# Gates and merges with tokens on the partitions, values behind the transposes, and a first product block tile by tile

## The chip, the core and the metric

The kernel runs on one core of a Trainium2 chip. Its metric is the device time of one execution in microseconds (us); the runs shown give 966.24, 966.26 and 968.72 us, median 966.26. The engines are named as in the profile: PE (TensorE, matmul), PEld (its weight load), DVE (VectorE), ACT (ScalarE), POOL (GpSimd) and SP (SyncE, which issues most DMAs).

## The reference, cut to what matters

Two transformer blocks stand one behind the other, on 256 tokens of width 1024, in float32. What the change touches:

```python
# block 1
z = rms_norm(x, norm1_w) @ w_in
(q, k_c, v_c, k_s, v_s, k_w, v_w, g_nsa, xr, gr, g_a, g_b) = split(z)
attn = nsa_attention(...)          # 8 heads: compressed, selected and windowed keys, gated
rnn  = rg_lru_branch(xr, gr, ...)  # conv, gates, scan over time, times gelu(gr)
merged = sigmoid(g_a) * (attn @ w_up_attn) + sigmoid(g_b) * (rnn @ w_up_rnn)
x = x + merged @ w_out             # then a feed-forward: square(relu(h @ mlp_w1)) @ mlp_w2
# block 2
h = h + 0.5 * swiglu(...)
qa, ka, va, qb, kb, vb, ga, gb = split(rms_norm(h) @ w_in_2)
ya = neighbourhood_attention_2d(qa, ka, va, rpb);  yb = windowed_gqa_sink(rope(qb), rope(kb), vb)
merged = sigmoid(ga) * (ya @ w_branch_a) + sigmoid(gb) * (yb @ w_branch_b)
h = h + merged @ w_out_2           # then a second swiglu and the last norm
```

## The kernel before

**Number format.** Each float32 operand is split in two parts of the fast matmul type, high and low: a copy on ACT gives the high part, a subtraction on DVE the low one (`split2`, L325; for weights `split_to`, L248 and L249). A product is then three matmuls, high by high, high by low and low by high. Weights arrive in pieces of up to 1024 columns (`raw`), are split into `whi` and `wlo` (five buffers each), and a piece is split two pieces ahead of its use (`wt`, L253). A buffer comes free when the last matmul that reads it is done.

**Layout.** Activations lie feature-major: 128 features on the partitions, 256 tokens along the free axis. `mmx` (L296) holds a weight tile of 128x128 and streams 256 tokens, three times. `mm3` (L290) is the other way about: a tile of activations (128 features by 128 tokens) is held and up to 512 weight columns are streamed, so that tokens come out on the partitions; before, the last down projection `ld` (L1483), `va` and `vg` use it. `mm_wide` (L302) streams high and low tokens together (512 columns) and then 256 for the low weights; the big feed-forwards and `wo` use it.

**Order.** Steps are recorded in the order of two lists, `ORDER_1` and `ORDER_2`, and a scheduler then sets the final order on each engine, which is fixed from there on. An entry such as `ga0` is one pair of output tiles of the gate g_a; `kv0` and `q0` are the first products of block 1; `ma0`..`mb3` are the two up projections; `at1` takes one attention step from a queue (scores, or transposes with the values straight behind them). Gates are evacuated by DVE (L984, times the norm's reciprocal), then go through tanh on ACT (L985). The merge multiplies (L1044), adds (L1050) and splits (L1051) each pair of tiles. PSUM is divided into pools: `g` three banks, `s` two, `t` two, `o` one.

**Start.** `setup` (L428) issues the DMA of the norm weights `vec` on ACT's queue, x in three DMAs and the first weight chunks between them on SP, and runs three warm-up matmuls `hot`. SP reuses eight DMA semaphores in turn, so a ninth DMA goes out when the first has landed.

Of the kernel before, what the change touches and what calls it, by code (L numbers as in the profile page):

```python
# [23 lines left out]
EARLY = 6  # L24
# [4 lines left out]
class Plan:  # L29
# [159 lines left out]
class Prog:  # L189
# [15 lines left out]
    def prepare(self):  # L205
# [32 lines left out]
    def split_to(self, i):  # L238
        nc = self.nc
        while self.n_split <= min(i, len(self.plan.pieces) - 1):  # L240
# [8 lines left out]
            nc.vector.tensor_tensor(out=lo[:, :w], in0=src, in1=hi[:, :w].bitcast(F32), op=ALU.subtract)  # L249
# [86 lines left out]
    def fm(self, tag, name, nk, npair, x, evac, rows=None, cols=None, lead=2, hold=2, after=None):  # L336
# [38 lines left out]
def build(nc, tc, d, out, es, dbg=None):  # L375
# [52 lines left out]
    def setup():  # L428
# [4 lines left out]
        for _ in range(3):  # L433
            nc.tensor.matmul(hb, hot[:, :P], hot, start=True, stop=True)
# [25 lines left out]
        for k in range(8):  # L460
            G.split2(*S["u0"].tile(k), res[:, k, :], V["norm1"][:, k:k + 1])
# [80 lines left out]
    def norm0():  # L542
        G.split_to(5)
        G.load_to(4)
        G.behind(nc.sync.dma_start(out=keep("ident", (P, P)), in_=d["ident"]), G.raw_ins[4])
        for p in range(4):
# [4 lines left out]
            G.behind(ins, G.hi_ins[5])  # L551
# [55 lines left out]
    def set_consts():  # L607
        G.load_to(6)
        G.behind(nc.sync.dma_start(out=S["vec2"], in_=d["vec2"]), G.raw_ins[6])
        G.behind(constants("cst1", CONST_1), G.raw_ins[6])  # L610

    def vg():
# [6 lines left out]
        hc = G.small((P, 2), "halfcol")  # L619
        nc.vector.tensor_scalar(out=hc, in0=S["colA"], scalar1=0.5, scalar2=None, op0=ALU.mult)  # L620
# [260 lines left out]
    def rnn_prep():  # L881
# [4 lines left out]
        nc.vector.tensor_tensor(out=tb, in0=ta, in1=V["lam"], op=ALU.min)  # L886
# [92 lines left out]
    def ev_tanh(key):  # L979
        def ev(p, b):  # L980
            if p == 0:
                S[key] = G.big(key)
# [599 lines left out]
```

## Time and profile before

| what | value |
|---|---|
| median of three runs | 966.26 us |
| the profiled execution | 966.17 us |
| its span, first to last instruction | 964.4 us |
| PE busy | 948.3 us, 98% of the span |
| DVE busy | 728.4 us, 76% |
| ACT busy | 585.0 us, 61% |

The difference of 1.8 us between the profiled time and its span lies outside the instructions. Busy is not idle-free work: a matmul's record is longer than the distance to the next one, since they are pipelined, so the cost of a matmul is read from start to start.

### The profile page before, as it was taken

What the parts mean: (1) busy time and instruction counts of PE and PEld (TensorE: products, weight loads), DVE (VectorE), ACT (ScalarE), POOL (GpSimd) and SP (SyncE); (2) the same over time, 40 slices, a digit from 0 to 9 for tenths busy, and PEclk for the clock granted to TensorE, in tenths of its full rate; (3) what the DMA queues carried; (4) which work ended last, traced back from release to release, by engine and by line L of the source; (5) the groups of instructions that cost most, each with busy time, mean ns of one, the idle gap of its engine ahead of it and who ended that gap; (6) DMA issues with size and microseconds to landing.
All of it is one profiled execution on the core that took longest, in us unless ns stands there. A gap on an engine that the chain in (4) does not pass through costs nothing.

```text
span 964.4 us, 15990 instructions
## 1 busy us (share of the span) xinstructions
PE 948.3 (98%) x6310; PEld 870.1 (90%) x6310; DVE 728.4 (76%) x1219; ACT 585.0 (61%) x961; POOL 42.0 (4%) x71
## 2 busy tenths in 40 slices
PE   8999999999999999999999999899999999999997
PEld 7989999998888888888888889899999888888897
DVE  7898879879888655679888657779767878777553
ACT  6795898546767544566555445678764565555441
POOL 6100000000000000030000200000000000000000
PEclk9999999999999999999999999999999999999999
DMA  9575442634545555565555755353334565555541
GB/s 331 188 268 212 138 154 104 245 131 178 215 175 193 201 177 196 195 207 180 203 187 182 240 180 177 136 204 108 113 132 172 178 201 204 185 175 183 186 141 45
DMA packets 26556, 174.03 MB, mean 180 GB/s; under 512 B 3313, under 2 KB 3569, under 8 KB 7281
## 3 DMA queue, kind: packets, MB, share of 16 engines
q1 hardware_dynamic: 24912, 169.80, 49.8%
q0 software_dynamic: 1136, 2.63, 1.4%
q8 instruction: 49, 0.80, 0.3%
q10 hardware_dynamic: 432, 0.58, 0.2%
q14 instruction: 27, 0.21, 0.1%
HBM read 171.43 MB, written 1.05 MB: 179 GB/s over the span
## 4 chain that ended last, share of the span: by engine, by line
PE 93%; ACT 4%; DVE 1%; issue 1%; DMA 0%; POOL 0%; POOLq 0%; ACTq 0%
PE f L306 17%; PE w L306 12%; PE f L307 9%; PE w L307 6%; PE ld L294 6%; PE ga L300 5%; PE fd L306 4%; PE gb L300 4%; PE wo L306 3%; PE m1b L300 2%; PE fd L307 2%; PE xr L300 2%; PE gr L300 2%; PE wo L307 2%; PE va L294 1%; PE ka L300 1%
## 5 line engine op out<-in xcount | busy, mean ns | idle before, releaser
L249 DVE TENSOR_TENSOR wlo<-raw,whi 128x1024 fp32r<-128x1024 f32 (+3 forms) x322 | 389.1, 1210 | 168.0 <-ACT whi L248 150.3
L248 ACT ACTIVATE whi<-raw 128x1024 fp32r<-128x1024 f32 (+3 forms) x322 | 335.7, 1047 | 285.6 <-PE w L306 64.2
L306 PE MATMUL f<-u,whi 128*128 128x512 f32 x704 | 246.7, 396 | 0.0
L307 PE MATMUL f<-u,wlo 128*128 128x256 f32 x704 | 196.5, 279 | 0.0
L306 PEld LDWEIGHTS f<-u,whi 128*128 128x128 f32 x704 | 132.0, 188 | 31.3
L307 PEld LDWEIGHTS f<-u,wlo 128*128 128x128 f32 x704 | 132.7, 188 | 0.1
L306 PE MATMUL w<-u,whi 128*128 128x512 f32 x256 | 88.8, 392 | 0.0
L306 PE MATMUL w<-hid,whi 128*128 128x512 f32 x256 | 88.8, 391 | 0.0
L307 PE MATMUL w<-hid,wlo 128*128 128x256 f32 x256 | 71.7, 280 | 0.0
L307 PE MATMUL w<-u,wlo 128*128 128x256 f32 x256 | 71.3, 280 | 0.0
L306 PE MATMUL fd<-f1h,whi 128*128 128x512 f32 x176 | 61.1, 394 | 0.0
L294 PE MATMUL ld<-whi,f2h 128*128 128x256 f32 (+1 forms) x264 | 59.0, 319 | 0.0
L306 PEld LDWEIGHTS w<-hid,whi 128*128 128x128 f32 x256 | 47.9, 187 | 10.5
L306 PEld LDWEIGHTS w<-u,whi 128*128 128x128 f32 x256 | 47.7, 187 | 10.3
L300 PE MATMUL ga<-u,whi 128*128 128x256 f32 x256 | 48.2, 284 | 1.1 <-ACT whi L248 1.1
L307 PE MATMUL fd<-f1h,wlo 128*128 128x256 f32 x176 | 48.8, 277 | 0.0
L307 PEld LDWEIGHTS w<-u,wlo 128*128 128x128 f32 x256 | 48.3, 189 | 0.2
L307 PEld LDWEIGHTS w<-hid,wlo 128*128 128x128 f32 x256 | 48.4, 189 | 0.0
L300 PE MATMUL gb<-u,whi 128*128 128x256 f32 x256 | 48.2, 284 | 0.0
L294 PEld LDWEIGHTS ld<-whi,f2h 128*128 128x128 f32 x264 | 44.0, 191 | 3.4
L306 PE MATMUL wo<-m,whi 128*128 128x512 f32 x128 | 44.3, 393 | 0.0
L294 PE MATMUL ld<-wlo,f2h 128*128 128x256 f32 (+1 forms) x132 | 42.1, 319 | 0.0
(533 smaller groups left out, 1924.5 us busy)
## 6 DMA issues: line engine op xcount, KB each, us to landing
raw<-in_ws_dram SPq DMA_DIRECT2D x150, 1024.0 KB, 4.8
raw<-in_ws_dram SPq DMA_DIRECT2D x3, 960.0 KB, 4.8
raw<-in_ws_dram SPq DMA_DIRECT2D x2, 992.0 KB, 4.9
nar<-in_rpb_dram POOLq DMA_DIRECT2D x16, 96.0 KB, 6.0
raw<-in_ws_dram SPq DMA_DIRECT2D x4, 256.0 KB, 6.4
raw<-in_ws_dram SPq DMA_DIRECT2D x2, 512.0 KB, 7.0
raw<-in_ws_dram SPq DMA_DIRECT2D x1, 932.0 KB, 5.1
res<-in_x_dram SPq DMA_DIRECT2D x2, 384.0 KB, 6.2
```

Source lines behind the costliest of these rows:

```text
L248: self.hi_ins.append(nc.scalar.activation(out=hi[:, :w], in_=src, func=AF.Copy))
L249: nc.vector.tensor_tensor(out=lo[:, :w], in0=src, in1=hi[:, :w].bitcast(F32), op=ALU.subtract)
L294: mm(out, a, b, start=start and r == 0, stop=stop and r == 2, skip_group_check=True)
L300: mm(out, a, b, start=start and r == 0, stop=stop and r == 2, skip_group_check=True)
L306: mm(bank.rearrange("p (a t) -> p a t", a=2), wh, x, start=start, stop=False, skip_group_check=True)
L307: mm(bank[:, :T], wl, x[:, 0, :], start=False, stop=stop, skip_group_check=True)
```

## The change

**Token-major gates and merges.** `tok` replaces the feature-major products of all four gates and all four up projections: an activation tile is held and 512 weight columns are streamed, tokens come out on the partitions. `ev_gate` needs no multiplication by DVE: the norm's reciprocal is a column per token and goes into ACT's tanh as its scale, straight from PSUM. In a part that ends a sum, the four weight tiles are held for both token halves (first all k of tokens 0 to 127, then all k of 128 to 255). The merged result must be turned back to feature-major for `wo`: 32 transposes on PE in all (16 per block), in `turn`; the split reads the turned tiles from PSUM. Half of a turn stands before the first product of `wo`, the other half (`mid`) between its later products; `wo` starts three pairs of output tiles instead of two before it closes the first.

**First products.** `kv0` and `q0` become one step, `first`, that goes through the eight k tiles and takes all four weight tiles of each; x and the weights come in eight DMAs each, alternating; the first weight chunk is issued on ACT's queue, `vec` on SP; the warm-up is two matmuls of 512 and 384 columns instead of three of 512. Tile 0 of `u0` (x times the norm weight) is split by DVE alone.

**Values behind transposes.** The attention queues take transposes and values as steps of their own, the values one or more steps later (`pv` in block 1, `v` in block 2).

**Other parts.** `qa` takes its PSUM banks from pool `s` instead of `g`; the mask of the neighbourhood bias becomes a step of its own (`nb`); a few small copies before the reciprocal root are dropped.

```diff
-EARLY = 6
+EARLY = 8
...
-ORDER_1 = """kv0 norm q0 cst kv_fin xr0 k0 q1 xr1 cmp_x cw0 cw1 cw2 vg0 cw3 prep cw4 at1 cw5 ga0 cw6 cw7 xr2 cmp_hT cmp_fin cmp_w2
...
+ORDER_1 = """norm cst xr0 kv_fin q_fin k0 q1 xr1 cmp_x cw0 cw1 cw2 vg0 cw3 prep cw4 at1 cw5 ga0 cw6 ga1 cw7 xr2 cmp_hT cmp_fin cmp_w2
+xr3 at1 ga2 cmp_attn ga3 at3 gr0 lru0 lru1 lru2 lru3 at1 gr1 at1 gr2 pv0 at1 gr3 exp sqrt bt at1 gelu gb0 pv0 at1 scan0 at1
+gb1 scan1 gb2 scan2 at2 scan3 gb3 at1 mb0 at1 mb1 pv0 at1 mb2 pv0 mb3 ma0 ma1"""
+ORDER_2 = """qs0 qs1 qe0 qe1 nb ka0 ka1 at1 va qb0 at1 qb1 at2 kb at3 ga0 at3 ga1 at3 ga2 at3 ga3 at3 gb0 at2 gb1 at2 gb2 at1
+ma0 gb3 ma1 mb0 mb1"""
...
+            if ci >= EARLY or ci % 4 == 0:
+                pool = "big" if ci < EARLY else "raw"
+                t = self.pools[pool].tile([P, 2 * PIECE], F32, tag=pool, name=f"raw{ci}")
+            else:
+                t = self.raw[ci - 1][:, PIECE // 2:]
+            queue = self.nc.sync if ci else self.nc.scalar
+            self.raw_ins.append(queue.dma_start(out=t[:, :w], in_=self.d["ws"][o:o + P * w].rearrange("(p w) -> p w", p=P)))
+            if ci > 1:
...
         if lead > 1 and hold:
             for p in range(lead):
                 part(p, 0, nk - hold)
+                if mid and p == 1:
+                    self.step(mid)
             for p in range(lead):
                 part(p, nk - hold, nk)
...
-        for _ in range(3):
-            nc.tensor.matmul(hb, hot[:, :P], hot, start=True, stop=True)
+        for n in (512, 384):
+            nc.tensor.matmul(hb[:, :n], hot[:, :P], hot[:, :n], start=True, stop=True)
...
-        nc.scalar.dma_start(out=vec, in_=d["vec"])
-        nc.sync.dma_start(out=res[:, 0:2, :], in_=d["x"][:, 0:2, :])
-        G.load_to(0)
-        nc.sync.dma_start(out=res[:, 2:5, :], in_=d["x"][:, 2:5, :])
-        G.load_to(1)
-        nc.sync.dma_start(out=res[:, 5:8, :], in_=d["x"][:, 5:8, :])
-        G.load_to(2)
+        nc.sync.dma_start(out=vec, in_=d["vec"])
+        for k in range(8):
+            nc.sync.dma_start(out=res[:, k:k + 1, :], in_=d["x"][:, k:k + 1, :])
+            G.load_to(k)
...
+            h, l = S["u0"].tile(k)
+            w = V["norm1"][:, k:k + 1]
+            if k:
+                G.split2(h, l, res[:, k, :], w)
+                continue
+            nc.vector.tensor_scalar(out=h, in0=res[:, k, :], scalar1=w, scalar2=None, op0=ALU.mult)
+            nc.vector.scalar_tensor_tensor(out=l, in0=res[:, k, :], scalar=w, in1=h.bitcast(F32), op0=ALU.mult, op1=ALU.subtract)
...
+    def tok(tag, name, c0, nk, x, ev, rows=None):
+        rows = rows or (lambda k: [(k * P, P)])
+        st = {}
+        def part(n):
+            c, h = divmod(n, nk // 4)
+            ks = range(4 * h, 4 * h + 4)
+            end = ks[-1] == nk - 1
+            def fn():
+                if h == 0:
+                    st[c] = [G.ps("g", f"{tag}{c}{i}") for i in range(2)]
+                ws = {k: G.wt((tag, k, c)) for k in ks} if end else None
+                for k, i in ([(k, i) for i in range(2) for k in ks] if end else [(k, i) for k in ks for i in range(2)]):
+                    wh, wl = ws[k] if end else G.wt((tag, k, c))
+                    xh, xl = (a[:, i * P:(i + 1) * P] for a in x(k))
+                    G.mm3(st[c][i], wh, wl, xh, xl, k == 0, k == nk - 1)
+                    if k == nk - 1:
+                        ev(c, i, st[c][i])
+            G.step(fn, [((tag, k, c), name, rows(k), [(c0 + c * 512, 512)]) for k in ks])
+        return part
...
+    def ev_gate(key, hc):
+        def ev(c, i, b):
+            if key not in S or S[key, "of"] != hc:
+                S[key] = G.big(key, shape=(P, 2, D))
+                S[key, "of"] = hc
+            nc.scalar.activation(out=S[key][:, i, c * 512:(c + 1) * 512], in_=b, func=AF.Tanh, scale=S["half" + hc][:, i:i + 1])
...
+    def take_values():
+        br, j = values.pop(0)
+        if br:
+            G.step(lambda: [nsa_cmp_pv(e) for e in (j - 1, j)])
+        G.step(lambda: nsa_pv(br, j // 2))
+        if br:
+            G.step(lambda: nsa_out(j // 2))
...
+    def first():
...
+            S["kcvc"], S["q0"] = G.ps("g", "kcvc0"), G.ps("s", "q0")
+            for k in range(8):
+                ws = [(S[key][:, nn * T:(nn + 1) * T], *G.wt((tag, k, nn)), nn) for key, tag in (("kcvc", "kcvc"), ("q0", "q"))
+                      for nn in range(2)]
+                x = xu(k)
+                for o, wh, wl, nn in ws:
+                    for a in range(2):
+                        nc.tensor.matmul(o, wh, x[:, a, :], start=k + nn + a == 0, stop=False, skip_group_check=True)
+                for o, wh, wl, nn in ws:
+                    nc.tensor.matmul(o, wl, x[:, 0, :], start=False, stop=k == 7, skip_group_check=True)
...
+        def ev(key):
+            def fn(c, i, b):
+                t = S[key][:, i, c * 512:(c + 1) * 512]
+                nc.vector.scalar_tensor_tensor(out=t, in0=t, scalar=1.0, in1=b, op0=ALU.add, op1=ALU.mult)
+                if (c, i) in done:
+                    fin(c, i)
+                done.append((c, i))
+            return fn
+        def fin(c, i):
+            t = S["tga"][:, i, c * 512:(c + 1) * 512]
+            nc.vector.tensor_tensor(out=t, in0=t, in1=S["tgb"][:, i, c * 512:(c + 1) * 512], op=ALU.add)
+            if (c, i) == (1, 0):
+                turn(0)
+        S[tag + "_turn"] = lambda: turn(1)
+        def turn(c):
             if tag not in S:
                 S[tag] = Parts(G.big, tag)
-            t = pair(S["tga"], p)
-            nc.vector.tensor_tensor(out=t, in0=t, in1=pair(S["tgb"], p), op=ALU.add)
-            G.split2(*S[tag].pair(p), t)
-
-        def branch(p, sfx):
-            w, nk, x, rows = ((wa, ka, xa, rows_a), (wb, kb, xb, rows_b))[sfx == "b"]
-            G.step(lambda: mm(p, sfx, nk, x, "tg" + sfx),
-                   [((tag + sfx, k, n), w, rows(k), [(n * P, P)]) for k in range(nk) for n in (2 * p, 2 * p + 1)])
-            if p in done:
-                G.step(lambda: fin(p))
-            done.append(p)
-
-        return branch
-
-    m1 = merge("m1", "w_up_attn", "w_up_rnn", 4, 8, lambda k: S["q"][:, :, k, :],
-               lambda k: S["rnn"].both(k), paired, plain)
+            for p in (2 * c, 2 * c + 1):
+                b = G.ps("t", f"{tag}T{p}")
+                for e in range(2):
+                    for i in range(2):
+                        f = (2 * p + e) * P
+                        nc.tensor.transpose(b[:, e * T + i * P:e * T + (i + 1) * P], S["tga"][:, i, f:f + P], S["ident"])
+                G.split2(*S[tag].pair(p), v2(b))
...
-    def out_proj(tag, name, x, fac, nxt):
+    def out_proj(tag, name, x, fac, nxt, mid):
...
-        G.fm(tag, name, 8, 4, x, ev)
+        G.fm(tag, name, 8, 4, x, ev, lead=3, hold=4, mid=mid)
...
+    def bias_mask():
+        S["nab"] = []
+        for hh, raw in enumerate(S["nar"]):
...
-    def z2(tag, c, p, ev, cols=None, ks=(0, 8), post=None):
+    def z2(tag, c, p, ev, cols=None, ks=(0, 8), post=None, pool="g"):
...
-                S[tag, p] = G.ps("g", f"{tag}{p}")
+                S[tag, p] = G.ps(pool, f"{tag}{p}")
...
-    def b2_tail(kind, j):
+    def b2_T(kind, j):
...
+    def b2_values(kind, j):
...
+    queue2 = [(kind, attn2[n_ - lag]) for n_ in range(11) for kind, lag in (("v", 3), ("t", 2), ("s", 0)) if 0 <= n_ - lag < 8]
...
+        "qs": lambda p: z2("qa", 0, p, ev_qa, ks=(0, 6), pool="s"), "qe": lambda p: z2("qa", 0, p, ev_qa, ks=(6, 8), post=None if p else mix_fin),
```

On DVE at the start of the program (`u` is x times the norm weight, `wlo_154` and `wlo_158` the low parts of the first and second weight chunk; before, 151 and 155), before:

```order
8 L333 SCALAR_TENSOR_TENSOR u_0_123<-res,vec,u_0_123 128x256 x2
9 L249 TENSOR_TENSOR wlo_151<-raw_114,whi_150 128x512
10 L333 SCALAR_TENSOR_TENSOR u_0_123<-res,vec,u_0_123 128x256
11 L895 RECIPROCAL sp_z<-sp_w 128x8
12 L333 SCALAR_TENSOR_TENSOR u_0_123<-res,vec,u_0_123 128x256
13 L333 SCALAR_TENSOR_TENSOR u_1_132<-res,vec,u_1_132 128x256
```

and of the change:

```order
6 L254 TENSOR_TENSOR wlo_154<-raw_113,whi_153 128x512
7 L254 TENSOR_TENSOR wlo_158<-raw_113,whi_157 128x512
8 L470 TENSOR_SCALAR u_0_131<-res,vec 128x256
9 L338 SCALAR_TENSOR_TENSOR u_0_131<-res,vec,u_0_131 128x256 x2
10 L471 SCALAR_TENSOR_TENSOR u_0_131<-res,vec,u_0_131 128x256
11 L254 TENSOR_TENSOR wlo_162<-raw_113,whi_161 128x512
```

Before, two `u` tiles stand ahead of the first chunk's low part and the second chunk's comes four rows later. Now the low parts of chunk 0 and chunk 1 stand ahead of the first `u` tile, whose own low part (L471) is fourth among the `u` rows.

On DVE at the end of block 1's merge (`m1a` are the banks of the last up projection, `m_0` the merged and split tile that the first product of `wo` reads, `wlo` splits of the weights that come next), before:

```order
320 L1044 SCALAR_TENSOR_TENSOR tga<-tga,m1a_2535 128x512
321 L1050 TENSOR_TENSOR tga<-tga,tgb 128x512
322 L249 TENSOR_TENSOR wlo_2702<-raw_2570,whi_2701 128x1024
323 L1044 SCALAR_TENSOR_TENSOR tga<-tga,m1a_2629 128x512
324 L249 TENSOR_TENSOR wlo_2736<-raw_2570,whi_2735 128x1024
325 L330 TENSOR_TENSOR m_0_2566<-tga,m_0_2566 128x512
326 L1050 TENSOR_TENSOR tga<-tga,tgb 128x512
327 L1044 SCALAR_TENSOR_TENSOR tga<-tga,m1a_2664 128x512
328 L249 TENSOR_TENSOR wlo_2758<-raw_2630,whi_2757 128x1024
329 L1050 TENSOR_TENSOR tga<-tga,tgb 128x512
330 L330 TENSOR_TENSOR m_0_2566<-tga,m_0_2566 128x512
```

and of the change:

```order
309 L1092 SCALAR_TENSOR_TENSOR tga<-tga,m1a_2307 128x512
310 L1100 TENSOR_TENSOR tga<-tga,tgb 128x512
311 L1092 SCALAR_TENSOR_TENSOR tga<-tga,m1a_2308 128x512
312 L1092 SCALAR_TENSOR_TENSOR tga<-tga,m1a_2347 128x512
313 L254 TENSOR_TENSOR wlo_2405<-raw_2275,whi_2404 128x1024
314 L1100 TENSOR_TENSOR tga<-tga,tgb 128x512 x2
315 L254 TENSOR_TENSOR wlo_2429<-raw_2313,whi_2428 128x1024
316 L1092 SCALAR_TENSOR_TENSOR tga<-tga,m1a_2348 128x512
317 L254 TENSOR_TENSOR wlo_2466<-raw_2313,whi_2465 128x1024
318 L335 TENSOR_TENSOR m_0_2378<-m1T_2373,m_0_2378 128x512
319 L335 TENSOR_TENSOR m_0_2378<-m1T_2381,m_0_2378 128x512
```

Before, the first half of `m_0` is split (row 325) while two more pairs of the up projection are still to come. Now both halves of `m_0` stand at the end, behind all four evacuations and three weight splits.

On PE in the same place of the change (`m1T` the turned tiles, rows 911 to 915 the last of the up projection):

```order
911 L299 MATMUL m1a_2348<-whi_2315,q_402 128x512
912 L299 MATMUL m1a_2348<-wlo_2316,q_402 128x512
913 L299 MATMUL m1a_2348<-whi_2315,q_402 128x512 x2
914 L299 MATMUL m1a_2348<-wlo_2316,q_402 128x512
915 L299 MATMUL m1a_2348<-whi_2315,q_402 128x512
916 L1115 MATMUL m1T_2373<-ident,tga 128x128
917 L1115 MATMUL m1T_2381<-ident,tga 128x128
918 L1115 MATMUL m1T_2373<-ident,tga 128x128 x3
919 L1115 MATMUL m1T_2381<-ident,tga 128x128 x3
920 L311 MATMUL wo_0_2402<-m_0_2378,whi_2349 128x512
```

The first product of `wo` (row 920) stands straight behind the eight transposes; before, it stood straight behind the last product of `m1a`.

On ACT in block 1, behind the square roots of the recurrence (`rg` the gelu, `tgb` the gate g_b, `gb` its bank), before:

```order
160 L268 ACT_TABLE_LOAD
161 L268 ACTIVATE rg<-rg 128x1024 x2
162 L329 ACTIVATE pt100h<-ptn_1892 128x384
163 L329 ACTIVATE pt101h<-ptn_1898 128x384
164 L248 ACTIVATE whi_2096<-raw_1835 128x1024
165 L248 ACTIVATE whi_2126<-raw_1955 128x1024
166 L985 ACTIVATE tgb<-tgb 128x512
167 L268 ACT_TABLE_LOAD
168 L268 ACTIVATE attn_1994,smn_1998<-attn_1994,nmn_1995 128x256 x2
```

and of the change:

```order
166 L273 ACT_TABLE_LOAD
167 L273 ACTIVATE rg<-rg 128x1024 x2
168 L273 ACT_TABLE_LOAD
169 L273 ACTIVATE attn_1876,smn_1880<-attn_1876,nmn_1877 128x256 x2
170 L253 ACTIVATE whi_1973<-raw_1832 128x1024
171 L253 ACTIVATE whi_2051<-raw_1832 128x1024
172 L334 ACTIVATE q_402<-o_0_1666 128x512
173 L334 ACTIVATE pt020h<-ptn_1899 128x384
174 L334 ACTIVATE pt021h<-ptn_1905 128x384
175 L334 ACTIVATE rnn_1892<-rg 128x512
176 L1020 ACTIVATE tgb<-gb_1814,halfcol_681 128x512
```

The tanh of the first gate banks reads PSUM now, and stands behind two table loads, the gelu, an attention's exponentials and two weight splits.

## Rows read from the trace of the kernel before

**Rows 1.** The page: busy time of the engines, and the chain's shares by engine.
```profile
PE 948.3 (98%) x6310; PEld 870.1 (90%) x6310; DVE 728.4 (76%) x1219; ACT 585.0 (61%) x961; POOL 42.0 (4%) x71
...
PE 93%; ACT 4%; DVE 1%; issue 1%; DMA 0%; POOL 0%; POOLq 0%; ACTq 0%
```
**Rows 2.** PE's waits: who waited for whom, us in total, times, longest.
```profile
PE ka L300 <- DVE qa L1255: 3.3, 1, 3.3
...
PE o L869 <- ACT pt100h L329: 0.2, 1, 0.2
```
**Rows 3.** The chain in order of time: start us, us, what, count.
```profile
20.80 1.44 PE xr L300 x12
...
149.92 5.27 PE gb L300 x44
...
671.26 0.87 PE pta L803 x8
```
**Rows 4.** Timeline of PE, 906 to 908 us: start us, us, instruction, count.
```profile
906.86 0.39 PE L294 MATMUL ld<-wlo,f2h 128*128 128x512 f32 x1
...
907.54 0.39 PE L294 MATMUL ld<-wlo,f2h 128*128 128x512 f32 x1
```
**Rows 5.** Stretches: us, PE, PEld, DVE, ACT, POOL busy (count), clock, DMA, GB/s.
```profile
610.00:614.00 4.00, 0.75 (x7) 0.55 (x5) 2.52 (x5) 1.33 (x3) 0.00 (x0) 1.00 0.40 124
614.00:617.00 3.00, 2.94 (x19) 2.97 (x20) 2.91 (x5) 2.90 (x5) 0.00 (x0) 0.73 0.78 325
617.00:620.00 3.00, 3.00 (x20) 3.00 (x20) 2.32 (x4) 2.88 (x6) 0.00 (x0) 0.70 0.03 5
```
**Rows 6.** Timeline of DVE and PE at the end of that stall.
```profile
613.23 1.28 DVE L1255 SCALAR_TENSOR_TENSOR qa<-qa,rb_A 128x512 f32<-128x512 f32 x2
614.06 0.47 PE L300 MATMUL ka<-u,whi 128*128 128x256 f32 x2 [3.31 <-DVE qa L1255]
```
**Rows 7.** Timeline of the start, 0 to 8 us.
```profile
1.46 4.29 PE L434 MATMUL hot<-hot 128*128 128x512 f32 x6 [1.46 <-DVE mhalf L440]
...
6.45 0.88 DVE L333 SCALAR_TENSOR_TENSOR u<-res,vec,u 128x256 fp32r<-128x256 f32 x2 [0.20 <-ACT u L332]
6.72 0.61 ACT L248 ACTIVATE whi<-raw 128x512 fp32r<-128x512 f32 x1
...
7.37 0.69 DVE L249 TENSOR_TENSOR wlo<-raw,whi 128x512 fp32r<-128x512 f32 x1
...
7.38 0.50 PE L300 MATMUL kcvc<-u,whi 128*128 128x256 f32 x2 [1.64 <-ACT whi L248]
```
**Rows 8.** Weight chunks' DMAs, issued at 1.19 and 2.12 us: KB, us to landing.
```profile
raw<-in_ws_dram SPq DMA_DIRECT2D x1, 256.0 KB, 4.5
...
raw<-in_ws_dram SPq DMA_DIRECT2D x1, 256.0 KB, 6.1
```
**Rows 9.** Stretch 40 to 60 us (columns as in rows 5).
```profile
40.00:60.00 20.00, 18.24 (x141) 16.93 (x140) 18.59 (x48) 19.75 (x45) 0.00 (x0) 1.00 0.56 197
```
**Rows 10.** Timeline of ACT, 141 to 160 us.
```profile
145.46 1.28 ACT L268 ACT_TABLE_LOAD   x1
146.76 2.01 ACT L268 ACTIVATE rg<-rg 128x1024 f32<-128x1024 f32 x2
148.67 0.47 ACT L329 ACTIVATE pt100h<-ptn 128x384 fp32r<-128x384 f32 x1
...
149.41 2.01 ACT L248 ACTIVATE whi<-raw 128x1024 fp32r<-128x1024 f32 x2
151.57 0.63 ACT L985 ACTIVATE tgb<-tgb 128x512 f32<-128x512 f32 x1
```
**Rows 11.** Timeline of DVE, 197 to 211 us.
```profile
203.18 0.68 DVE L1044 SCALAR_TENSOR_TENSOR tga<-tga,m1a 128x512 f32<-128x512 f32 x1
203.78 1.22 DVE L249 TENSOR_TENSOR wlo<-raw,whi 128x1024 fp32r<-128x1024 f32 x1
204.91 0.68 DVE L330 TENSOR_TENSOR m<-tga,m 128x512 fp32r<-128x512 f32 x1
```

More of the change, by code (lines that the diff above doesn't have):

```diff
@@ L223, in prepare @@
         self.hi_ins = []
+        self.lo_ins = []
         self.raw_ins = []
@@ L530, in norm_chain @@
     def norm_chain(v, name):
-        ss = G.small((P, 2), "ssc" + name)
-        nc.vector.tensor_copy(ss, v[:, :, 0])
-        r = rstd_of(ss, name)
+        r = rstd_of(v[:, :, 0], name)
         S["col" + name] = r
@@ L542, in norm0 @@
     def norm0():
-        G.split_to(5)
-        G.load_to(4)
-        G.behind(nc.sync.dma_start(out=keep("ident", (P, P)), in_=d["ident"]), G.raw_ins[4])
+        G.behind(nc.sync.dma_start(out=keep("ident", (P, P)), in_=d["ident"]), G.raw_ins[8])
         for p in range(4):
@@ L977, in rnn_scan, with half_col @@
         G.split2(*S["rnn"].pair(p), S["rg"][:, sl, :])
[L979 to L982, printed above, removed]
-            t = pair(S[key], p)
-            nc.vector.tensor_tensor(out=t, in0=v2(b), in1=two(S["rbA"]), op=ALU.mult)
-            nc.scalar.activation(out=t, in_=t, func=AF.Tanh, scale=0.5)
+    def tok(tag, name, c0, nk, x, ev, rows=None):
[17 more added lines that the diff above has]
+        return part
+    def half_col(name):
+        hc = G.small((P, 2), "halfcol" + name)
+        nc.vector.tensor_scalar(out=hc, in0=S["colA"], scalar1=0.5, scalar2=None, op0=ALU.mult)
+        S["half" + name] = hc
+    def ev_gate(key, hc):
[4 more added lines that the diff above has]
+            nc.scalar.activation(out=S[key][:, i, c * 512:(c + 1) * 512], in_=b, func=AF.Tanh, scale=S["half" + hc][:, i:i + 1])
         return ev
@@ L1035, in merge @@
         done = []
-        def mm(p, sfx, nk, x, key):
-            b = G.ps("g", f"{tag}{sfx}{p}")
-            for k in range(nk):
-                for nn in range(2):
-                    wh, wl = G.wt((tag + sfx, k, 2 * p + nn))
-                    G.mmx(b[:, nn * T:(nn + 1) * T], wh, wl, x(k), k == 0 and nn == 0, k == nk - 1)
-            t = pair(S[key], p)
-            nc.vector.scalar_tensor_tensor(out=t, in0=t, scalar=1.0, in1=v2(b), op0=ALU.add, op1=ALU.mult)
-        def fin(p):
+        def ev(key):
[6 more added lines that the diff above has]
+            return fn
@@ L1074, in build @@
+        "gb": gb, "cw": cmp_w1, "lru": lru, "scan": lambda p: G.step(lambda: rnn_scan(p)),
+        "ma": m1a, "mb": m1b, "at": lambda n: [take() for _ in range(n)]}
+    STEPS_1 = {"q_fin": lambda: ev_q(0, S["q0"]), "norm": norm0, "kv_fin": kcvc_fin, "cst": set_consts, "prep": rnn_prep, "cmp_x": cmp_x, "cmp_hT": cmp_hT, "cmp_fin": cmp_fin, "cmp_w2": cmp_w2, "cmp_attn": cmp_attn,
                "exp": rnn_exp, "sqrt": rnn_sqrt, "bt": rnn_bt, "gelu": rnn_gelu}
+    first()
     for w in ORDER_1.split():
@@ L1238, in bias_load @@
                                         in_=bass.AP(base.tensor, o, [[1, 64], [127, 6], [1, 64]]))
+        sk = keep("sink", (P, 8))
+        nc.gpsimd.dma_start(out=sk, in_=d["rows"][0, 0:8].partition_broadcast(P))
+    def bias_mask():
+        S["nab"] = []
+        for hh, raw in enumerate(S["nar"]):
             nb = G.big(f"nab{hh}", shape=(P, 4, 6, 64))
@@ L1242, in bias_load @@
                                     in1=raw[:, :, ::-1], op=ALU.subtract)
-        sk = keep("sink", (P, 8))
-        nc.gpsimd.dma_start(out=sk, in_=d["rows"][0, 0:8].partition_broadcast(P))
     def mix_fin():
         norm_fin("acc1", "A")
+        half_col("2")
         for k in ("cos", "sin"):
```

107 lines of the change are left out of this document (38 added, 69 removed).

## The prediction

> **What bounds the kernel now.** I read the page first. PE is busy 98% of the span and holds 93% of the chain [rows 1]: PE's order of work is the time, and other engines count only where PE waits for them. So the second view is PE's waits. Few are left: one of 3.3 us at `ka`, for `qa` banks that DVE has still to empty, and small ones, the last 0.2 us at `o` [rows 2]. Hence two sums. One is PE work removed and added, start to start, since the records overlap. The other is waits removed and made, and for these it is read which row now stands last ahead of a PE instruction, and whether PE has work enough before it.
>
> **Prices.** A product that streams 256 columns: 44 in 5.27 us, 0.120 us each; transposes: 8 in 0.87, 0.109 each [rows 3]. One that streams 512 columns: three steps from 906.86 to 907.54, 0.227 each [rows 4]. Two products of 256 cost 0.240, so one of 512 saves 0.013. DVE at work without a break steps 0.60 us for 128x512 and 1.13 for a weight split of 128x1024 [rows 11]. From DVE's end to PE's start lies 0.2 us: the first `qa` row of two ends at 613.23 + 0.64 = 613.87, `ka` starts at 614.06 [rows 6].
>
> **1. Products.** Four gates of 192 matmuls each: 768 x 0.120 becomes 384 x 0.227, that is 92.2 to 87.2, -5.0. The four up projections: 480 become 240, 57.6 to 54.5, -3.1. 32 transposes of 0.109 are new, +3.5. Net -4.6.
>
> The row says 0.109 for a transpose, at full clock. The Trainium skill ("TensorE: Matmul & The Clock Gate", section "Part 4: PE-mode transpose") measured some 275 ns in one kernel and says that transposes don't keep the clock up; by it the 32 would cost 8.8 instead of 3.5. These rows speak against it.
>
> **2. The `ka` stall.** With `qa` in pool `s`, `ka`'s second bank pair waits for nothing: -3.3. The stall is dearer than that: behind it the granted clock is 0.73 and 0.70 for two stretches of 3 us [rows 5]. A share c is 2c - 1 of the time at full speed and the rest at half, so 0.27 x 3 + 0.30 x 3 = 1.7 us is lost, counted as work not done at full speed. Gone with the stall: -5.0 together. The cover is `ka`'s own second half, 48 products x 0.120 = 5.8 us from 610.4, while DVE has emptied `qa` by 614.5 [rows 6]. Late next is pool `s`: two `qa` pairs, the first scores and the second column half of `va` now take its two banks in turn, and that half runs as a pass of its own which holds five weight pieces. Nothing before shows this; below 0 it cannot go, above lies one evacuation of 1.28 [rows 6] and one weight split of 1.13 [rows 11], 2.5. I take +1.5, near the evacuation.
>
> **3. The start.** Before, the warm-up ends at 5.75 and the first product runs at 7.38, held by `whi` of chunk 0 and the split behind it; `kv0` and `q0` are through at 20.80 [rows 3, 7]. Now DVE's order puts the low parts of chunks 0 and 1 ahead of the first `u` tile, so the first product needs chunk 1. Counted in KB issued up to and with it, that is the 824th (`vec` 56, x 128, 256, 128, 256). Chunks landed at 5.7 (568 KB: `vec`, 256 of x, 256) and 8.2 (1208) [rows 8], so 824 lands near 6.7. Then `whi` 0.61, `wlo` 0.69, `u` high some 0.44 (half of 0.88) [rows 7]: first product 8.5 at the earliest. The second operand, `u` low, stands three DVE rows later, 0.88 + 0.44: 9.9. From there 94 products x 0.120 = 11.3 give 21.2, +0.4 against 20.80. The bounds are 0 and 1.1, the lateness of the first product. The warm-up is shorter, 896 of 1536 columns x 4.29 = 2.5 us, and ends near 4.0, so PE stands idle 4.5 us. The stall of 3.3 us halved the clock and cost 1.7. This one is longer: I take +1.7 (0 to 1.7).
>
> The Trainium skill ("TensorE: Matmul & The Clock Gate", section "Why this matters for your kernels") also warns that a gap between bursts of matmuls puts the clock back to its lower level; rows 5 agree, with 0.73 and 0.70.
>
> **4. 40 to 66 us.** ACT is busy 19.75 us of 20 and DVE 18.59 [rows 9]; transposes and values as separate steps, and gates that wait for ACT, move rows here. No row prices a new order of the same work. Bounds -1 (ACT cannot get shorter than what PE waits for there) and +2 (one pair of weight splits, 2.01 [rows 10]); I take +1.0.
>
> **5. `gb`.** Before, DVE emptied the `gb` banks. Now ACT's tanh does, behind two table loads (2 x 1.28), the gelu (2.01), two exponentials, q and a half of rnn (four rows of about 0.5), two weight splits (2.01), two `pt` (2 x 0.47) and its own 0.63: 10.2 us by durations; rows in a run overlap by 0.1 (146.76 + 2.01 against 148.67), so about 9.2 [rows 10]. PE has, between the first `gb` pair and the next, 30 products x 0.227, 14 x 0.120 and 6 transposes x 0.109 = 9.1. If ACT enters on time the wait is 0 to 1.1, and each weight split of 1.0 that it is behind adds as much: 0 to 2.5, taken +1.5.
>
> **6. `wo`, the end of block 1's merge.** After the bank `m1a_2307` PE has 20 products x 0.227 + 8 transposes x 0.109 = 5.4 us. DVE has to do, by its order up to the first split of `m_0`, seven rows of 0.60, three weight splits of 1.13 and 0.69: 8.3, and a hand-off at either end, 0.3: 8.6. PE waits +3.2. Before, half of `m_0` was split two pairs earlier and there was no wait here [rows 2]. Bounds: 0, if the weight splits come later than they stand, to 4.3, one more split. The wait is as long as the one that halved the clock, so +1.5 (0 to 1.7) for that.
>
> **7. `wo2`, the same place in block 2.** From about 0.7 us before the last product DVE has 1.13 + 0.60 + 1.13 + 0.69 = 3.5; PE has 0.7 and six transposes, 0.65: +2.2 (0 to 3.0).
>
> **8.** The wait at `o` goes as values follow their transposes later: -0.2 [rows 2]. The dropped copies, the mask as a step of its own and the further rows of DVE and ACT lie beside PE work and cost nothing; tanh from PSUM takes 128x512 multiplications off DVE where it is not late. If that cover fails it shows as more of items 4 and 5.
>
> **Sum.** -4.6 - 5.0 + 1.5 + 0.4 + 1.7 + 1.0 + 1.5 + 3.2 + 1.5 + 2.2 - 0.2 = +3.2. It is made on the profiled execution, 966.17 (span 964.4 and 1.8 around it), 0.1 below the median of 966.26: 969.4.
>
> **Rivals.**
> - *Merges in time.* If DVE's splits at both merges are done when PE's last transpose is, items 6 and 7 fall away: 969.4 - 3.2 - 1.5 - 2.2 = 962.5. It decides at the first product of `wo`: DVE must do 8.3 us of rows in 5.4. For it: gates no longer take DVE, so earlier weight splits may be done sooner. Against: the banks' evacuations cannot start before PE is done with them, and DVE's order is fixed.
> - *More half clock.* The waits at `gb` and `wo2`, each above 1, grow to where the clock falls, 1.7 us each: 972.8. For it: a 3.3 us wait did it [rows 5]. Against: both are shorter than 3.3, and no wait of 1 to 3 us in these rows is seen to do it.
> - *The stall moves.* `qa` in pool `s` only hands the wait on, and the change does not do what it says: +5.0, 974.4. For it: pool `s` has two banks against three. Against: the evacuation is over before 5.8 us of products are.
> - *An easy start.* Tile by tile, PE runs from the first chunk and no clock is lost: -2.1, 967.3. Against: DVE's order.
> - *Dear transposes.* Those that stand between products, not eight in a row, take as long as a product of 512, 0.227 [rows 4]: 32 x 0.118 = +3.8, 973.2. Against: [rows 3]. By the Trainium skill's figure, named in item 1, it would be +5.3 and 974.7, an estimate.
>
> **Chances.** Forecast 0.38, merges in time 0.20, more half clock 0.15, stall moves 0.12, easy start 0.12, dear transposes 0.03. About 0.3% (2.9 us) is what a measurement here can tell from no change, so 963.4 to 969.2. Forecast (own range 967.0 to 972.0): slower 0.21, same 0.17; merges in time: faster 0.13, same 0.07; easy start: same 0.09, slower 0.03; the other three slower, 0.30. Together faster 0.13, same 0.33, slower 0.54. The range 961.5 to 974.5 leaves out some of the first and the last rivals and holds the bounds of single items.
>
> **What would show it.** Item 1: PE's records of `ga` to `m1a` fewer, start to start 0.227, transposes 0.109. Item 2: no `ka` in PE's waits, granted clock 1.00 behind it; wrong if `va`, `ka` or scores wait for `qa` over 2 us. Item 3: first product near 8.5, `xr` near 21 to 23, clock below 1 in the first 15 us. Items 5 to 7: PE's waits name `gb` by ACT's tanh, `wo` and `wo2` by DVE's `m_0` row, near 1.5, 3.2 and 2.2, and the clock behind `wo` below 1. If `wo` waits under 1 us, the forecast is wrong on the fast side; if several stretches stand near 0.7, on the slow side.

## The result, and the profile after

The change makes the kernel slower, by 1.1%: median 977.62 us (four executions, 976.35 to 979.71) against 966.25; ratio 1.0114, 95% interval 1.0100 to 1.0128. The forecast was 969.4. The profiled execution took 977.98, its span is 976.2, again 1.8 us outside the instructions; the span grew by 11.8.

The page's busy times of the changed kernel, which answer to [rows 1]:

```profile
PE 953.1 (98%) x5716; PEld 844.2 (86%) x5716; DVE 721.9 (74%) x1202; ACT 588.9 (60%) x962; POOL 38.1 (4%) x71
```

PE has 594 records fewer and is busy 4.8 us longer. Its waits (who for whom, us in total, times, longest), to be held against [rows 2]:

```profile
PE wo L311 <- DVE m L335: 5.1, 2, 3.1
PE kcvc L1073 <- DVE u L470: 3.6, 1, 3.6
...
PE ga L299 <- ACT whi L253: 1.2, 1, 1.2
PE gb L299 <- ACT tgb L1020: 1.1, 1, 1.1
PE kcvc L1073 <- DVE u L471: 0.6, 1, 0.6
PE pta L806 <- DVE pta20l L335: 0.5, 1, 0.5
PE vg L299 <- DVE q L583: 0.5, 1, 0.5
```

The 3.3 us at `ka` are gone, and the waits the prediction named are there: 3.1 at `wo`, 2.0 at `wo2` (5.1 in two), 1.1 at `gb`, 3.6 ahead of the first product. The end of block 1's merge on DVE, first the timeline of DVE, then of PE, in the change:

```profile
204.81 0.69 DVE L1092 SCALAR_TENSOR_TENSOR tga<-tga,m1a 128x512 f32<-128x512 f32 x1 [1.31 <-PE m1a L299]
...
210.80 0.68 DVE L1092 SCALAR_TENSOR_TENSOR tga<-tga,m1a 128x512 f32<-128x512 f32 x1
211.40 1.22 DVE L254 TENSOR_TENSOR wlo<-raw,whi 128x1024 fp32r<-128x1024 f32 x1
212.54 0.69 DVE L335 TENSOR_TENSOR m<-m1T,m 128x512 fp32r<-128x512 f32 x1
```
```profile
209.14 1.03 PE L1115 MATMUL m1T<-ident,tga 128*128 128x128 f32 x8
213.28 0.50 PE L311 MATMUL wo<-m,whi 128*128 128x512 f32 x1 [3.10 <-DVE m L335]
```

From 204.81 to 213.23 DVE works without a break, 8.4 us (8.3 were reckoned), while PE is through its last transpose at 210.17. The granted clock (in a row of stretches the value behind the five busy times) in the change at the start and behind the wait at `wo`:

```profile
8.00:10.00 2.00, 0.93 (x4) 0.76 (x5) 2.00 (x6) 2.00 (x6) 0.00 (x0) 0.72 1.07 397
10.00:12.00 2.00, 2.00 (x11) 2.00 (x11) 2.00 (x5) 1.73 (x4) 0.00 (x0) 0.50 1.14 377
12.00:14.00 2.00, 2.00 (x12) 2.00 (x11) 1.88 (x5) 0.98 (x3) 0.00 (x0) 0.50 0.98 405
14.00:17.00 3.00, 3.00 (x20) 3.00 (x20) 0.89 (x2) 1.05 (x2) 0.00 (x0) 0.71 1.03 431
...
212.00:216.00 4.00, 2.72 (x9) 2.39 (x10) 2.42 (x4) 0.00 (x0) 0.00 (x0) 0.71 0.74 252
216.00:220.00 4.00, 4.00 (x22) 3.44 (x22) 0.00 (x0) 0.00 (x0) 0.00 (x0) 0.86 0.21 90
```

At the start 0.28 x 2 + 0.50 x 4 + 0.29 x 3 = 3.4 us of work are lost, at `wo` (0.29 + 0.14) x 4 = 1.7; part of the 3.4 passes while PE still waits for its second operand. Where the clock stands at 0.50, products of 256 columns start 0.213 us apart, in place of 0.120.

All that makes some 7 of the 11.8 us. The rest shows in no wait. It is in products that the change does not touch: block 1's feed-forward (`w`) and block 2's first swiglu (`f`, and `fd` for its down projection), which the expectations below count as the second feed-forward of block 1. First the kernel before, then the change, groups of products from 300 to 310 us (count | busy, mean ns of one | idle):

```profile
L306 PE MATMUL w<-u,whi 128*128 128x512 f32 x30 | 10.4, 391 | 0.0
```
```profile
L311 PE MATMUL w<-u,whi 128*128 128x512 f32 x30 | 10.6, 399 | 0.0
```

Same instruction, no idle time, clock 1.00, yet 8 ns longer. Such products come in pairs, one of 512 columns and one of 256. The distance from the start of one pair to the start of the next, called the pace from here on, is 346.7 ns before and 353.3 in the change, with nothing between (the records overlap, so busy time over count gives it too: 10.4 / 30 and 10.6 / 30 us). The change stays at 353.3 nearly all the way from 239 to 607 us; from 802 us, in block 2's last feed-forward, it runs at 346.7, where the kernel before has 353.3 from 788 us on.

Where the time went, summed from each PE product's start to the next one's, by the name of the tile that it writes (block 1: `Sn` scores, `vg` values, `cmph` the compression; block 2: `Sa` scores, `pta` and `ptb` turned probabilities, `va` values, `qb` queries):

| item of the prediction | forecast | measured |
|---|---|---|
| 1 gates, without `gb`'s wait | -5.0 | -3.5 |
| 1 up projections; transposes | -3.1; +3.5 | -2.9; +3.3 |
| 2 stall at `ka` with its half clock | -5.0 | -5.0 |
| 2 pool `s` (`va`, `Sa`, `pta`, `qb` in block 2) | +1.5 | +2.9 |
| 3 start | +2.1 | +3.0 |
| 4 40 to 66 us (`Sn`, `vg`, `cmph`, the wait at `ga` behind it) | +1.0 | +1.3 |
| 5 `gb`'s wait | +1.5 | +1.1 |
| 6 `wo`: wait; half clock | +3.2; +1.5 | +3.1; +1.7 |
| 7 `wo2`'s wait | +2.2 | +2.0 |
| 8 `o` | -0.2 | -0.4 |
| pace of `w`, `f`, `fd`, `wo` | 0 | +4.8 |
| longer single steps in `wo` and `wo2`, beside waits and transposes | 0 | +0.8 |
| all other names | 0 | -0.4 |

In the row of the pace `w` is +3.2, `fd` +1.2, `wo` +0.3; `f` loses 2.0 in block 2's first swiglu and gains 1.9 in its last.

### The profile page after: what moved, and what is told of

It reads as the page before. It is cut to its first block, busy times and chain, and to the rows that moved or that the text cites. A ratio compares the mean times of both kernels' runs of the same rounds, so it can differ in the third digit from the quotient of the medians.

```text
span 976.2 us, 14789 instructions
## 1 busy us (share of the span) xinstructions
PE 953.1 (98%) x5716; PEld 844.2 (86%) x5716; DVE 721.9 (74%) x1202; ACT 588.9 (60%) x962; POOL 38.1 (4%) x71
## 5 line engine op out<-in xcount | busy, mean ns | idle before, releaser
L254 DVE TENSOR_TENSOR wlo<-raw,whi 128x1024 fp32r<-128x1024 f32 (+2 forms) x324 | 388.9, 1204 | 176.2 <-ACT whi L253 156.9
L253 ACT ACTIVATE whi<-raw 128x1024 fp32r<-128x1024 f32 (+2 forms) x324 | 336.2, 1043 | 287.8 <-PE w L311 66.2
L311 PE MATMUL wo<-m,whi 128*128 128x512 f32 x128 | 47.1, 411 | 5.2 <-DVE m L335 5.1
L299 PE MATMUL gb<-whi,u 128*128 128x512 f32 x128 | 42.2, 396 | 1.1 <-ACT tgb L1020 1.1
L299 PE MATMUL ga<-whi,u 128*128 128x512 f32 x128 | 42.0, 397 | 1.2 <-ACT whi L253 1.2
```

The costliest lines, as they stand in the source:

```text
L253: self.hi_ins.append(nc.scalar.activation(out=hi[:, :w], in_=src, func=AF.Copy))
L254: self.lo_ins.append(nc.vector.tensor_tensor(out=lo[:, :w], in0=src, in1=hi[:, :w].bitcast(F32), op=ALU.subtract))
L299: mm(out, a, b, start=start and r == 0, stop=stop and r == 2, skip_group_check=True)
L311: mm(bank.rearrange("p (a t) -> p a t", a=2), wh, x, start=start, stop=False, skip_group_check=True)
```

## The experiments

**The pace, interrupted in some 60 places.** `NUDGE` goes through eight small groups of idle PE instructions.

```diff
+        if self.n_pair % 24:
+            return
+        cols, ones = NUDGE[self.n_pair // 24 % len(NUDGE)]
...
+            self.nc.tensor.transpose(b[:, 128 + n * P:256 + n * P], idt, idt)
```

> The changed kernel with a few idle PE instructions (one to three transposes, one to four products of two columns) behind every 24th pair of wide products, some 60 places, nothing left out; about 15 us of added work. The trace of the change shows a pair of 512 and 256 columns at 353.3 ns from 239 to 607 us and at 346.7 ns from 802 us; before it is 346.7 nearly everywhere and 353.3 from 788 us. Theory A (phase): the pace has two values and every interruption of the stream draws anew, so both 346.7 and 353.3 are seen all over block 1, changing at the added instructions. Theory B (place): the pace belongs to where the tiles of a stage lie in memory, so block 1's first feed-forward stays at 353.3 and the last one at 346.7, whatever interrupts.

One execution: 1004.91 us, 27 above the change where 15 were reckoned. All over the stages that ran at 353.3 both paces are found, and they change at the added instructions, here at two products of two columns. Timeline of PE in this run:

```profile
293.82 0.39 PE L329 MATMUL w<-u,whi 128*128 128x512 f32 x1
294.05 0.28 PE L330 MATMUL w<-u,wlo 128*128 128x256 f32 x1
294.17 0.39 PE L329 MATMUL w<-u,whi 128*128 128x512 f32 x1
...
295.90 0.28 PE L320 MATMUL nudge<-ones,ident 128*128 128x2 f32 x2
296.04 0.48 PE L329 MATMUL w<-u,whi 128*128 128x512 f32 x1
...
296.47 0.40 PE L329 MATMUL w<-u,whi 128*128 128x512 f32 x1
...
297.18 0.40 PE L329 MATMUL w<-u,whi 128*128 128x512 f32 x1
```

Pairs start 0.35 apart ahead of it and 0.355 behind (two in 0.71), and the rows of two stretches show the two means, 289 to 295 and 297 to 303 us:

```profile
L329 PE MATMUL w<-u,whi 128*128 128x512 f32 x19 | 6.6, 391 | 0.0
...
L329 PE MATMUL w<-u,whi 128*128 128x512 f32 x18 | 6.4, 399 | 0.0
```

Both lie in one stage, which reads the same tensors throughout. Theory B (place) falls.

**The change once more.**

> The changed kernel once more, unaltered. If the pace is a matter of the program (its timing or its addresses), the same stages run at 353.3 ns a pair, 239 to 607 us, and the time is 977 to 978. If each execution draws it, some stages come out at 346.7 and the time lies up to 6 us lower or 2 us higher.

One execution, 975.57 us, below the 977 to 978 expected; but every stage is at the same pace as in the first profile: in two executions of one program the pace is the same. What differs is the clock. Behind the wait of 3.1 us at `wo` it stays up here, and `wo` takes 1.6 us less. At the start PE stood idle 4.1 us (3.6 in the first). The row of the stretch shows a clock of 1.00 there, but the trace holds no record of the clock before 12.9 us, and the timeline of PE tells another story:

```profile
8.00:17.00 9.00, 7.72 (x49) 7.45 (x50) 7.77 (x16) 6.22 (x14) 0.00 (x0) 1.00 1.03 384
```
```profile
11.50 0.63 PE L1075 MATMUL kcvc<-u,wlo 128*128 128x256 f32 x2
11.92 0.63 PE L1075 MATMUL q<-u,wlo 128*128 128x256 f32 x2
...
13.56 0.40 PE L1075 MATMUL kcvc<-u,wlo 128*128 128x256 f32 x2
13.80 0.40 PE L1075 MATMUL q<-u,wlo 128*128 128x256 f32 x2
```

Two products of 256 columns take 0.42 us from start to start up to 12.8 us, the price of half clock, and 0.24 from 13.1 on. So half clock cost time at the start here too. Steps of 0.213 stand in all five profiled executions of the change's start with its warm-up of 512 and 384 columns, up to 12.8 to 15.7 us. The two profiled executions differ by 2.4 us: 1.6 at `wo` and 0.9 at the start. That the spread of the others, 976.3 to 979.7, has the same cause is likely, but not shown: the trace tells of the profiled execution alone.

**`qa` in pool `s` alone.**

```diff
-        "qs": lambda p: z2("qa", 0, p, ev_qa, ks=(0, 6)),
+        "qs": lambda p: z2("qa", 0, p, ev_qa, ks=(0, 6), pool="s"),
```

> The kernel before with one part of the change alone: qa takes its banks from pool s. My item 2: the wait of 3.3 us at ka and the half clock behind it go, 966.3 - 5.0 = 961.3, and the pool's new users cost 0 to 2.5, so 961 to 964. Rival (the stall moves): 966, with a wait of about 3 us at another name. By theory A a change of pace in single stages may add up to 6 us that no wait shows.

961.77 us (961.72 to 961.81), ratio 0.9950 (0.9935 to 0.9965): 4.5 us. No `ka` in PE's waits, and the stretch of the old stall:

```profile
610.00:620.00 10.00, 10.00 (x80) 10.00 (x79) 9.78 (x16) 9.03 (x13) 0.00 (x0) 1.00 0.64 208
```

The stall does not move. `va` is 0.1 us longer, `qb` 0.4, `Sa` and `pta` not at all: alone, the pool costs 0.5 of the +2.9 in block 2 of the change, and the rest comes with the other parts.

**The merges' ends in another order.**

```diff
-            if (c, i) == (1, 0):
+            if (c, i) == (0, 1):
                 turn(0)
...
+                        if c:
+                            G.behind(ins[0], S["turned"] if i else st["end"])
...
-ma0 gb3 ma1 mb0 mb1"""
+ma0 mb0 gb3 ma1 mb1"""
```

> The changed kernel with both merges' ends set out otherwise: in block 2 mb0 stands before gb3; the first half of a turn follows as soon as the first 512 columns are merged, and in block 1 the second column half is kept behind the first, with the eight transposes between its two token halves. If the waits of 3.1 and 2.0 us at wo and the half clock behind (1.8) come from DVE's order there, they go: 977.6 - 6.9 = 970.7. If they come from the transposes as such, they stay near 5 us and the time is 977.

971.08 us (971.00 to 971.23). Of the two waits this is left:

```profile
PE wo L313 <- DVE m L337: 0.3, 1, 0.3
```

The order at the merges' ends made them; the transposes, all of which are still there, cost what a row says. The half clock behind `wo` is gone too.

**The old start.** The functions `setup`, `norm0`, `load_to` and the two steps as before; nothing else.

```diff
-ORDER_1 = """norm cst xr0 kv_fin q_fin k0
+ORDER_1 = """kv0 norm q0 cst kv_fin xr0 k0
```

> The changed kernel with the start of the kernel before: kv0 and q0 one behind the other, six half chunks, x in three transfers, three warm-up products; all else of the change stays. The trace of the change has xr at 23.6 us against 20.6; of these 3.0 up to 3.4 are half clock from 8.6 to 16 us, and a second execution without that half clock took 2.4 us less. Theory (idle PE and late first operand cost it): 977.6 - 3.0 = 974.6, within 973.5 to 975.5, xr near 20.7. Rival (the loss is the later work's, which collides anyway at 40 to 66 us): 977.

975.61 us (972.92 to 978.05): -2.0, where -3.0 was expected; the runs overlap with the change's. In the profiled execution `xr` starts at 21.6, not 20.7, since PE waits 1.4 us for a weight split within the first products. The time saved is not waited for later: PE waits 1.6 us at `cmph` instead of 0.4, but `Sn`, `vg` and `ga` are shorter by 2.6, and `gb` starts 3.5 us ahead of the change (134.1 for 137.6). So the later work does not swallow the gain, as the rival had it. Half clock behind `wo2`, which the change's profiled execution does not have, then takes 1.7 of it back.

**One more transpose in each of two feed-forwards.**

```diff
+        if self.n_pair in (136, 668):
+            self.nc.tensor.transpose(self.ps("t", "nudge")[:, :P], S_ALL["ident"], S_ALL["ident"])
```

> The changed kernel with two more transposes on PE and nothing else: one in the first feed-forward of block 1 and one in the next, each behind the norm's own small products. In the run with some 60 additions a single transpose was followed by 346.7 ns a pair in seven places of seven. Theory A (pace by phase): some 870 pairs then take 6.67 ns less, -5.8 + 0.2 = -5.6: 972.0. Theory B, or no lasting effect: 977.8.

974.45 us (972.69 to 976.34), -3.2, where -5.6 was expected. The first, at 264.2 us, left `w` as it was. `f` and `fd` run at the fast pace and take 3.1 us less, but not by the second, which comes at 453.2: `f` is fast before it. Rows of 300 to 310, 441 to 450 and 500 to 510 us:

```profile
L319 PE MATMUL w<-u,whi 128*128 128x512 f32 x30 | 10.6, 399 | 0.0
...
L319 PE MATMUL f<-u,whi 128*128 128x512 f32 x27 | 9.4, 391 | 0.0
...
L319 PE MATMUL f<-u,whi 128*128 128x512 f32 x30 | 10.4, 391 | 0.0
```

In the change the row of 441 to 450 us has 399. Up to the second transpose the two programs differ on the engines by the first alone. It did not change the pace behind it, but at 439 us, behind the small products of the norm that both programs have, `f` took up 346.7 here and 353.3 there, and kept it through `fd`, some 165 us. An instruction of 0.1 us can thus decide a pace 175 us later; what the second did is not shown.

**`qa` in pool `s` and one transpose.** The same line, at pair 1224 of the kernel before.

> The kernel before with qa in pool s, and one more transpose on PE in the last feed-forward, behind its norm's small products. There the trace shows 353.3 ns a pair for 49 groups of six pairs, 784 to 890 us. Theory A: 49 x 6 x 6.67 ns = -2.0 + 0.1, so 961.8 - 1.9 = 959.9. Theory B: 961.9.

961.94 us (961.84 to 963.71): nothing gained, the pace stays at 353.3. A single transpose is no reset, as I had taken it from seven places of seven; those lay a multiple of 24 pairs behind the interruption ahead of them, and the slow pace repeats every three pairs, so they may all have met it at one place of its cycle.

**A longer warm-up in the change.**

```diff
-        for n in (512, 384):
+        for n in (512,) * 4:
```

> The changed kernel with a warm-up of four products of 512 columns instead of 512 and 384, ending near 7.2 us instead of 4.8, so that PE is idle 1.3 us and not 3.6 before the first product at 8.45. If that idle time is what halves the clock, the granted clock of the first 20 us is 1.00, and the time is 974 to 976 in every run (the change spread from 976.3 to 979.7). If the half clock has another cause, 977 to 980 stays; if the warm-up keeps PE from its work, later than that.

980.59 us (978.28 to 983.69), not the 974 to 976 expected; the median is 3.0 above the change's, but the runs overlap with the change's. The clock at the start does stay up: products of 256 columns start 0.120 apart from 9.8 us on, and `xr` begins at 20.9, not 23.6, with the second operand at the same time (9.53). So half clock at the start cost the change 2.7 us in its first profile, and 1.3 in the second, where `xr` begins at 22.7 and the second operand came 0.5 later. Then PE, earlier, runs into the weight splits; stretches and PE's longest wait there:

```profile
8.00:17.00 9.00, 7.94 (x64) 7.77 (x65) 7.17 (x16) 6.05 (x13) 0.00 (x0) 1.00 1.04 383
48.00:52.00 4.00, 2.85 (x14) 2.41 (x15) 4.00 (x14) 3.90 (x9) 0.00 (x0) 0.84 0.40 166
52.00:56.00 4.00, 4.00 (x27) 3.99 (x27) 3.39 (x8) 3.94 (x10) 0.00 (x0) 0.73 0.23 37
...
72.00:76.00 4.00, 4.00 (x13) 3.11 (x12) 1.95 (x11) 0.92 (x1) 0.58 (x4) 0.67 0.62 242
```
```profile
PE cmph L676 <- ACT whi L253: 1.8, 1, 1.8
```

Behind the waits the clock is at half twice, and the 2.7 us gained at `xr` are 2.5 lost at `gb` (140.1 for 137.6). An early `xr` alone does not make this loss: with the old start it comes at 21.6, and `gb` keeps the gain. Which part of the new start does it was not taken apart.

**Three transposes, seven pairs apart.** As the run with one, at pairs 1224, 1231 and 1238.

> The kernel before with qa in pool s and three single transposes in the last feed-forward, seven pairs apart, instead of the one that left it at 353.3 ns. The slow pace shows as a cycle of three pairs (241+120, 236+113, 233+117 ns). Theory A, made sharper: what an interruption does hangs on the place in that cycle where it falls; seven pairs apart the three fall on three places, so at least one leads to 346.7 and the last 47 groups of six pairs take 6.67 ns a pair less: 961.8 - 1.9 + 0.3 = 960.2. If it stays at 353.3: 962.1.

960.41 us (960.10 to 961.66), ratio 0.9934 (0.9920 to 0.9949), as expected to 0.2 us. The last feed-forward is fast from 792 us; its rows of 820 to 830 us, first with one transpose, then with three:

```profile
L314 PE MATMUL f<-u,whi 128*128 128x512 f32 x30 | 10.6, 399 | 0.0
```
```profile
L314 PE MATMUL f<-u,whi 128*128 128x512 f32 x30 | 10.4, 391 | 0.0
```

It is the fastest kernel of the study. Its profiled execution shows steps of 0.213 at the start too, from 8.9 to 12.1 us; the other six profiled executions with the start of the kernel before show none later than 7.6 us.

**All of it on the change.** Old start, merges' order, three transposes in each of two feed-forwards.

> Towards a version that beats both: the changed kernel with the old start, the merges' ends as in the run on their order, and three transposes in each of block 1's two feed-forwards. From 971.1 (merges' order): old start -1 to -3, pace -5.4 + 0.6: 962 to 966. If the pace stays slow: 968 to 970. Against 961.8 of the kernel before with qa's pool alone.

962.34 us (962.19 to 963.23). `w`, `f` and `fd` run at the fast pace from the transposes on. Against `qa`'s pool alone, sums by name give gates -2.3, up projections -2.5, transposes +2.8: 2.0 gained of the 4.6 of item 1, 1.1 of the difference being `gb`'s wait. `pta`, `va` and `Sa` take +2.4, so that all of it comes out about even; that the gates and merges make these three longer is not shown.

**Values straight behind the transposes again.**

```diff
-            G.step(lambda: (b2_T if kind == "t" else b2_values)(br, j))
+            G.step(lambda: [b2_T(br, j), b2_values(br, j)])
```

> As the run before it on this chip, with values straight behind the transposes again in both blocks (the orders of the kernel before, gates and merges as in the change). If the waits at vg, va, pta and Sa, some 3 us in the change, come from the values' new places, it is 2 to 3 us faster than that run; if they come from the weights' order and the gates, the two are the same within 1 us.

966.13 us (965.64 to 966.64), 3.8 slower than the run before it. But `f` and `fd` (+2.8) are at the slow pace in this program, in spite of three transposes; without that it is 1.0 us. `pta` gains 0.8, `ptb` loses 2.0, `cmph` 1.8, `gb` gains 2.3. Of the first theory only `pta` is left: `va` and `Sa` do not move, and `va`'s waits remain, for the weights' splits and for the masking of the first scores. The second holds only with the pace taken off, and which row makes `va` and `Sa` longer is not shown.

## Why the prediction was wrong

- The direction was right and the size was not: +11.8 between the two profiled executions, on which the sum was made (+11.4 by medians), for +3.2. **The step that failed is the first, the prices:** they were read from rows of before and taken as fixed for every product that the change leaves alone, so that these entered the sum as nothing. They have two paces 6.67 ns a pair apart, and the change happened to set the slow one from 239 to 607 us. That is 4.8 of the 8.6 us missed. No rival had it. The run with two transposes shows what it costs: `f` and `fd` are fast there, 3.1 us less by name, hardly anything else differs, and its median is 3.2 lower. Why the change met the slow pace stays open.
- Most of the other 3.8 us: gates 1.5, the row of pool `s` 1.4, the start 0.9, longer steps in `wo` and `wo2` 0.8.
- Items 2 (the stall), 6, 7 and 8 are right to 0.2 us, and by their mechanism: the run on the merges' order takes both waits away, the run on `qa`'s pool the stall. The rivals "merges in time" and "the stall moves" fall. So does "dear transposes": all 32, those between products too, took 3.3 us, and about 0.1 more for the product behind a group. Eight took 1.03 us; the record of a single one lasts 0.27, so the other seven step by 0.109: item 1 sets a duration against a distance.
- "More half clock" did not come at `gb` or `wo2` in the profiled execution; behind `wo2`'s wait of 2.0 us it did in two of the six profiled executions that have this wait. "An easy start" falls with the first product at 8.45 us.
- Item 1's gates were mis-sized: 3.5 saved for 5.0. Of their 384 products 22 step by 0.29 us or more where 0.227 was reckoned, 2.3 us in all, and 126 by 0.23 to 0.24, 0.8 us; before, 18 of 768 were long, 1.6 us. What holds them is not shown. The up projections, by the same price, came out right.
- Item 3: the first product came at 8.45 (8.5 forecast), the second operand at 9.54 (9.9). The warm-up was scaled from one whose last records of 512 columns step by 0.43 us; in the shorter one every step is of 0.85, so that it took 3.36 us, not 2.5. Half clock at the start was mis-sized: 2.7 us in one execution and 1.3 in another, for 1.7. The Trainium skill ("TensorE: Matmul & The Clock Gate", section "Why this matters for your kernels") warns of such gaps; the first profile agrees: behind 3.6 us idle the granted clock falls to 0.50. In the second, behind 4.1, the products ran at half clock, but no record tells whether the clock had risen before.
- Item 2's +1.5 for pool `s` was too much: 0.5 where the pool alone is changed. The other 2.4 of the +2.9 in block 2 belong to moved rows there: 0.8 to the place of the values (`pta`), 0.4 to a wait of `va` for the masking of the first scores; the rest stays open.
- Item 4 was of the right size (+1.0, measured 1.3) by luck. It was put down to transposes and values as separate steps and to gates that wait for ACT; `ga`'s wait was there before (1.1 us, now 1.2), and with the old start and all else of the change as it is, `Sn`, `vg` and `cmph` together lie within 0.2 us of the kernel before. The new start made it.

## What to carry to other kernels

Before pricing a change, look at whether products that it does not touch keep their distance, start to start; a kernel bound by PE can lose or gain several us there with no wait in the profile. Take a change of many parts apart: here one word, the pool of `qa`, was worth 4.5 us, and the rest cost 16. What a part gains at its place can be lost behind it: 2.7 us of an earlier start were gone 120 us later in the run with the longer warm-up, while the 2.0 us of the old start were kept. Where the view of the clock shows 1.00 at the start of a program, check it against the distance of two equal products.

## What the runs showed of the hardware

- A stream of alternating products of 512 and 256 columns settles on 346.7 or on 353.3 ns a pair at full clock and keeps it until something else comes between, some instructions of 0.1 us being enough; then it may settle on the other. The slow one repeats every three pairs (241+120, 235+114, 232+118 ns). For one program it was the same in two executions. Both were found within one stage, so it does not hang on where the tiles of a stage lie. What picks it is open: behind three transposes it was the fast one in four stretches (two in the run with all of it, one each in the fastest kernel and in the run with values straight) and the slow one in a fifth, and one transpose changed what a later, equal interruption picked.
- At the start of the change, with the short warm-up and 3.6 to 4.1 us idle behind it, products of 256 columns stepped by 0.213 us, half clock, in all five profiled executions, until 12.8 to 15.7 us; with a longer warm-up and 0.9 us idle they stepped by 0.120.
- Behind the wait of 3.1 us at `wo` the clock was at half in four of six profiled executions, and behind the wait of 2.0 us at `wo2` in two of six: the same wait does it in some executions and not in others. In the first profile it cost 1.7 us at `wo`.
